# One opening, four visits: loads moved to GpSimd's queue, a bias load moved behind half of B, put-aside sums in A's tiles, and ten sums of B drawn forward

## The chip, the core and the metric

The kernel runs on one core of a Trainium2 chip. The metric is the device time of one execution in microseconds (us). The engines of the core have short names in the profile: PE is the matrix engine (PEld its weight loads), DVE the vector engine, ACT the scalar engine, POOL is GpSimd, SP is the sync engine, which here only issues DMAs. DMAs are issued by SP and by POOL, each on a queue of its own; the transfers of both queues run on the same 16 DMA engines of the core.

## What is computed

```python
def setup_inputs():
    m, k, n = 4096, 4096, 4096
    return {
        "a": np.random.randn(m, k).astype(np.float32),
        "b": np.random.randn(k, n).astype(np.float32),
        "bias": np.random.randn(n).astype(np.float32),
    }

def reference(a, b, bias):
    return np.tanh(np.matmul(a, b) + bias)
```

All three inputs are fp32. The kernel casts A and B to fp16 while they are loaded (a cast in a DMA is issued on POOL's queue) and accumulates in fp32.

## The kernel before

**Tiling.** The output is cut into four column stretches of 1024 (two halves j of 512) and into 32 row tiles of 128. K is 4096, cut in two halves h of 16 steps t each; a step is 128 deep. Most of the work is done by a seven-product scheme (`PRODUCTS`, `product`, L278): a pair of row tiles and the two halves of K and of the columns make a 2x2 block problem, and seven products of sums of A's quadrants (`asum`: s1, s2, s5, s6, s7) with sums of B's quadrants (`bsum`: d3, d1, d4, e6, e7, each in four blocks of four steps) replace eight. Work between the products is put by hand into numbered slots (`at_slot`, seven slots to an item); an engine runs its instructions in the order in which this program writes them.

**The opening.** The sums of B don't exist at the start, so the first eight row tiles (m 0 to 3 are `g0`, 4 to 7 are `g1`) of the first column stretch are multiplied plainly (`mm`, L425, 512 matmuls of 128x512) in four visits, so that PE can begin with what has landed. Eight PSUM banks hold `mb[m % 4, j]`.

1. Visit one: `g0`, steps 0 to 3 of the first half of K. A's piece for it is `first`, four loads of 128 KB, turned by PE (`turn_first`, L528) and copied out by DVE and ACT (L530). ACT puts the eight sums aside in `spill[0..3]` (`put_aside`, L461).
2. Visit two: `g1`, steps 0 to 7; A comes by `land` (L475, POOL's queue) and is turned by DVE (`turn_in`, L173). ACT puts the sums aside in `spill[4..7]`; DVE copies `spill[0..3]` back into PSUM (L571).
3. Visit three: `g0`, steps 4 to 15. ACT puts the sums aside, again in `spill[0..3]`; DVE writes `spill[4..7]` plus bias into PSUM (`add_bias`, L85, eight instructions). These are the first instructions that read the bias tile `bias_bc`.
4. Visit four (`second_visit`, slots -20 to -1): `g1` to its end (slots -20 to -9), with tanh and store (`end`, L596); ACT copies `spill[0..3]`, to which DVE has added the bias in slots -16 to -14, back into PSUM (L611); then `g0`, steps 16 to 31 (slots -8 to -1). The sums of B for the first items of the seven-product scheme, and the turned A of item 0, are made beside it on DVE. Slot 0 starts the first product of item 0.

**Queues.** POOL issues, in this order: `first` (4 DMAs); four single-step loads of b11 and b12 (t = 2, 3); `land` g1a0, g1a1 (8); block 1 of b11 and b12 (8); `land` g0b (4); block 2 (8); `land` g0x0, g0x1 (8); block 3 (8); `land` g1x0, g1x1 (8); `land` g1c 0 to 3 (16); the second half of B, b21 and b22, in the block order 2, 0, 1, 3 (32); `land` g0c (16); then A for items 0, 1, and so on (`load_nat`). The DMAs of this queue share eight semaphores in turn, so that each waits until the one eight before it has landed. SP issues at the start: four loads of t = 0, 1 of b11 and b12 in fp32 (`early_b`, 256 KB each), which DVE (L511) and ACT (L512) cast into the fp16 tiles, and then the bias, one row of 4 KB copied to 128 partitions (512 KB written, L260).

**Tiles that are shared.** A tile with a tag takes the place of the tile that had this tag before, once all that read it are done. `spill[0..3]` have the tags of e7's four blocks (`SPILL[0]`), `spill[4..7]` those of block 1 of d3, d1, d4, e6 (`SPILL[1]`; `early_b` has two of these before it). A's tiles of `g0` (`aq[m, 0]` and `aq[m, 1]`) lie in the pool `quads` under a11, a21, a12, a22, two each, which items 0 and 1 use after them.

**The sums of B, before.** d3, d1 of block 2 in slot -13; d4, e6 of block 2 in -12; d3, d1, d4 of block 0 in -11; d3 of block 3 in -8; e7 of block 0 in -7; e6 of block 0 in -6; e7 of block 2 in -5; d1, d4, e6 of block 3 in -3, -2, -1; d3 of block 1 and e7 of block 3 in 0; d1, d4, e6, e7 of block 1 in 2, 3, 5, 7.

Of the kernel before, what the change touches and what calls it, by code (L numbers as in the profile page):

```python
# [8 lines left out]
P = 128  # L9
QP = 32  # L10
NB = 512
NCW = 2 * NB
T = 16
TB = 4
# [3 lines left out]
fp32 = mybir.dt.float32  # L18
fp16 = mybir.dt.float16
# [29 lines left out]
SPILL = (  # L49
    [f"e7_{blk}" for blk in range(4)],  # L50
    [f"{i}_1" for i in ("d3", "d1", "d4", "e6")],
)
# [4 lines left out]
def kernel(  # L57
# [7 lines left out]
    nc = tc.nc  # L65
# [8 lines left out]
    bops = ctx.enter_context(tc.tile_pool(name="bops", bufs=1))  # L74
    quads = ctx.enter_context(tc.tile_pool(name="quads", bufs=2))
    sums = ctx.enter_context(tc.tile_pool(name="sums", bufs=3))
    wide = ctx.enter_context(tc.tile_pool(name="wide", bufs=8))
# [146 lines left out]
    bop, raw = {}, {}  # L224

    def new_bop(name, blk):
        bop[name, blk] = bops.tile([P, TB, NB], fp16, name=f"{name}_{blk}", tag=f"{name}_{blk}")
        return bop[name, blk]

    def load_b(dst, c, blk, h, j, t0=0, nt=TB, one=None):  # L230
        dx, dt = (1, QP) if h or blk else (TB, 1)
        off = b.offset + (h * T * QP + blk * TB * QP + t0 * dt) * N + c * NCW + j * NB
        if nt == 1:
            src = bass.AP(tensor=b.tensor, offset=off, ap=[[KQ * N, 4], [dx * N, QP], [1, NB]])
            (one or nc.gpsimd).dma_start(out=dst if one else dst[:, t0, :], in_=src)
            return
        for q in (0, 2, 1, 3):
            src = bass.AP(
                tensor=b.tensor, offset=off + q * KQ * N, ap=[[dx * N, QP], [dt * N, nt], [1, NB]]
            )  # L240
            nc.gpsimd.dma_start(out=dst[ds(q * QP, QP), ds(t0, nt), :], in_=src)  # L241

    def load_raw(name, c, blk):
        raw[name, blk] = wide.tile([P, TB, NB], fp16, name=name, tag="wide")
        load_b(raw[name, blk], c, blk, *((0, 1) if name == "b12" else (1, 0)))

    def load_op(name, c, blk):
        load_b(new_bop(name, blk), c, blk, *((0, 0) if name == "b11" else (1, 1)))
# [6 lines left out]
        x, y = (bop[i, blk] if (i, blk) in bop else raw[i, blk] for i in (x, y))  # L255
        tt(new_bop(name, blk), x, y, op)

    def load_bias(c):
        src = bias[ds(c * NCW, NCW)]
        nc.sync.dma_start(  # L260
            out=bias_bc, in_=bass.AP(tensor=src.tensor, offset=src.offset, ap=[[0, P], *src.ap])
        )

# [95 lines left out]
    def at_slot(slot, f, *args):  # L359
        work.setdefault(slot, []).append((f, args))  # L360
# [47 lines left out]
    def opening_b(names, blk, t0=0, nt=TB):  # L408
        for name in names:
            if t0 == 0:  # L410
                if name in ("b11", "b22"):
                    new_bop(name, blk)
                else:
                    raw[name, blk] = wide.tile([P, TB, NB], fp16, name=name, tag="wide")
            dst = bop[name, blk] if name in ("b11", "b22") else raw[name, blk]
            load_b(dst, 0, blk, int(name[1]) - 1, int(name[2]) - 1, t0, nt)
# [6 lines left out]
    def mm(m, j, kt, start=False, stop=False):  # L423
        h, t = divmod(kt, T)
        nc.tensor.matmul(  # L425
            mb[m % 4, j], aq[m, h][:, t, :], right(kt, j),
            start=start, stop=stop, skip_group_check=True,
        )

    def across(ms, k0, k1, fresh=False):  # L430
        for kt in range(k0, k1):
            for m in ms:
                for j in range(2):
                    mm(m, j, kt, fresh and kt == k0)

    def down(m, j, k0, k1, fresh=False, stop=False):
        for kt in range(k0, k1):
            mm(m, j, kt, fresh and kt == k0, stop and kt == k1 - 1)
# [6 lines left out]
    for m in g0:  # L445
        for h in range(2):
            name = f"a{m % 2 + 1}{h + 1}"
# [4 lines left out]
    spill = {}  # L452
# [7 lines left out]
    def put_aside(m, j):  # L460
        nc.scalar.copy(spill[m, j], mb[m % 4, j])  # L461

    def add_bias(m, j, to):
        tt(to, spill[m, j], bias_bc[:, ds(j * NB, NB)], ADD)
# [3 lines left out]
    def land(key, m, k0, nk, tag, nrow=1):  # L468

        h, t0 = divmod(k0, T)  # L470
        pool = sums if tag == "sum" else bops
        tl = pool.tile([P, 4 * nrow, nk * QP], fp16, name="land", tag=tag)
        for q in (0, 2, 1, 3):
            src = a[ds(m * P, nrow * P), ds(q * KQ + h * T * QP + t0 * QP, nk * QP)]
            nc.gpsimd.dma_start(  # L475
                out=tl[ds(q * QP, QP)], in_=src.rearrange("(mb p) k -> p mb k", p=QP)
            )
        landed[key] = (tl, m, k0, nk)
# [18 lines left out]
    for m in g0:  # L497
        src = a[ds(m * P, P), :].rearrange("p (q k) -> p q k", q=4)[:, :, ds(0, TB * QP)]
        nc.gpsimd.dma_start(out=first[:, m], in_=src)  # L499
    nc.gpsimd.affine_select(  # L500
        out=ident, in_=ident, compare_op=mybir.AluOpType.is_equal, fill=0.0,
        base=0, pattern=[[-1, P]], channel_multiplier=1,
    )
    early_b = [bops.tile([P, 2, NB], fp32, name="early_b", tag=SPILL[1][t]) for t in range(2)]
    new_bop("b11", 0)
    raw["b12", 0] = wide.tile([P, TB, NB], fp16, name="b12", tag="wide")
    for t in range(2):
        for j in range(2):
            load_b(early_b[t][:, j], 0, 0, 0, j, t, 1, nc.sync)
    for t in range(2):  # L510
        nc.vector.tensor_copy(bop["b11", 0][:, t], early_b[t][:, 0])  # L511
        nc.scalar.copy(raw["b12", 0][:, t], early_b[t][:, 1])  # L512
    for t in range(2, TB):
        opening_b(("b11", "b12"), 0, t, 1)
    land("g1a0", 4, 0, TP, "sum", 2)
    land("g1a1", 6, 0, TP, "sum", 2)
# [21 lines left out]
    def turn_pairs(key):  # L538
        for p in range(2):
            for r in range(2):  # L540
                turn_in(f"{key}{p}", r)
# [33 lines left out]
        down(m, j, TB, TP)  # L575
    turn_pairs("g0x")
    land(("g1c", 3), 7, T, T, LAND[1])
    for blk in H1:
        opening_b(("b21", "b22"), blk)
    load_bias(0)  # L580
    across(g0, TP, T - 2)
    turn_pairs("g1x")
    for m, j in rows4:
        down(m, j, T - 2, T, stop=True)
        put_aside(m, j)
        add_bias(4 + m, j, mb[m, j])

# [33 lines left out]
    for i, (m, j) in enumerate(rows4):  # L621
        at_slot(-16 + i // 3, add_bias, m, j, spill[m, j])
    for slot, name, blk in (
        (-13, "d3", 2), (-13, "d1", 2), (-12, "d4", 2), (-12, "e6", 2),
        (-11, "d3", 0), (-11, "d1", 0), (-11, "d4", 0), (-8, "d3", 3), (-7, "e7", 0),
        (-6, "e6", 0), (-5, "e7", 2), (-3, "d1", 3), (-2, "d4", 3), (-1, "e6", 3),
        (0, "d3", 1), (0, "e7", 3), (2, "d1", 1), (3, "d4", 1), (5, "e6", 1), (7, "e7", 1),
    ):
        at_slot(slot, bsum, name, blk)

# [3 lines left out]
    for c in range(1, NC):  # L634
        n = next(n for n in range(len(items)) if items[n][0] == c)
        change(c, 0, n - 2)
        change(c, 1, n - 1)
        at_slot(SLOTS * (n - 1) + 3, load_bias, c)
# [39 lines left out]
```

## Time and profile before

| what | value |
|---|---|
| median of 3 runs | 1601.43 us (1601.06 to 1601.47) |
| the profiled execution | 1598.97 us, of which its span is 1597.2 us |
| PE busy | 1571.0 us, 98% of the span, 7259 matmuls |
| DVE, ACT, POOL busy | 918.0, 268.6, 384.2 us (57%, 17%, 24%) |
| DMA on POOL's queue | 85.51 MB written, 36.5% of 16 engines' span |
| DMA on SP's queue | 173.05 MB, 33.0% |
| mean granted clock of PE | 0.993 |

A line of the timeline gives start, duration, engine, line, operation, tiles and a count, and in brackets the idle time of the engine ahead of it with what ended it. A line of the table of windows gives, for a stretch, the busy time and the number of instructions of PE, PEld, DVE, ACT and POOL, then the granted clock, the share of the DMA engines and GB/s written. The chain of waits is followed back from the last instruction; each piece is a start, a duration and what it was. Beside these views the trace has, for every DMA, the time at which each of the 16 DMA engines reported its part done; "landed" below is the last of these 16.

### The profile page before, as it was taken

Reading aid. Unit: us, or ns where it says so; the run is one execution under the profiler, and the core shown is the slowest. Engines: PE = TensorE matmul, PEld = TensorE weight load, DVE = VectorE, ACT = ScalarE, POOL = GpSimd, SP = SyncE. Lnnn points to the kernel's source line nnn. Section 1 sums busy time; section 2 is a strip of 40 time slices with the busy share of each in tenths; the row PEclk is TensorE's granted clock in tenths of the full one; section 3 lists DMA queues with packets and bytes.
Section 4 is the critical chain, followed back from the end, with each engine's and each line's share of the span. In section 5 each row is a group of like instructions: output and inputs, shape, how many; then the busy total and the mean of one; then the engine's idle time right before and its main releaser. Section 6 shows DMA issues by size and latency. Waiting matters only on the chain.

```text
span 1597.2 us, 18918 instructions
## 1 busy us (share of the span) xinstructions
PE 1571.0 (98%) x7259; PEld 710.3 (44%) x7259; DVE 918.0 (57%) x1044; ACT 268.6 (17%) x475; POOL 384.2 (24%) x721
## 2 busy tenths in 40 slices
PE   5998999999999999999999999999999999999998
PEld 2444444444444444444444444444444444444443
DVE  1769777777885665577795333333369433334332
ACT  1221111111221111111122111111122211111111
POOL 4765434364532221146441000000140000000000
PEclk7999999999999999999999999999999999999999
DMA  8999978899978765599996444444494444444441
GB/s 126 187 212 232 203 174 176 176 196 224 192 168 234 184 160 157 164 220 224 215 166 171 121 131 139 121 135 132 134 191 117 145 139 132 125 139 130 121 143 49
DMA packets 163114, 259.76 MB, mean 163 GB/s; under 512 B 24784, under 2 KB 83664, under 8 KB 163024
## 3 DMA queue, kind: packets, MB, share of 16 engines
q0 software_dynamic: 93376, 85.51, 36.5%
q1 hardware_dynamic: 69648, 173.05, 33.0%
q8 instruction: 57, 0.93, 0.2%
q14 instruction: 33, 0.27, 0.1%
HBM read 243.27 MB, written 100.66 MB: 215 GB/s over the span
## 4 chain that ended last, share of the span: by engine, by line
PE 93%; DMA 4%; POOL 1%; issue 1%; DVE 1%; ACT 0%; DVEq 0%; POOLq 0%
PE ps L278 90%; PE ps L425 3%; DMA nat<-in_a_dram 2%; DMA b<-in_b_dram 2%; POOL land L475 0%; POOL b L241 0%; DMA land<-in_a_dram 0%; POOL first L499 0%; DVE a L173 0%; DVE oa L173 0%; POOL nat L145 0%; ACT o L596 0%; ACT ps L611 0%; DVE s L85 0%; DVE d L85 0%
## 5 line engine op out<-in xcount | busy, mean ns | idle before, releaser
L278 PEld LDWEIGHTS <-a 128*128 128x128 f16 x3648 | 356.9, 98 | 433.4 <-issue 3.1
L278 PEld LDWEIGHTS <-s 128*128 128x128 f16 x3072 | 300.6, 98 | 364.0 <-issue 1.7
L278 PE MATMUL ps<-d,a 128*128 128x512 f16 x1920 | 434.0, 379 | 2.8 <-DVE ps L85 2.8
L278 PE MATMUL ps<-b,s 128*128 128x512 f16 x1920 | 434.0, 379 | 1.4 <-DVE s L85 1.4
L278 PE MATMUL ps<-e,a 128*128 128x512 f16 x1728 | 390.4, 379 | 0.0
L85 DVE TENSOR_TENSOR s<-a,a 128x2048 f16<-128x2048 f16 x192 | 233.1, 1215 | 13.1 <-DMA a<-scratch 12.1
L241 POOL DMA_DIRECT2D b<-in_b_dram x248 | 133.7, 547 | 434.4 <-PE ps L278 362.4
L145 POOL DMA_DIRECT2D nat<-in_a_dram x272 | 142.1, 534 | 314.1 <-DVE a L173 254.3
L278 PE MATMUL ps<-d,s 128*128 128x512 f16 x960 | 217.0, 379 | 0.0
L173 DVE STREAM_TRANSPOSE a<-nat 128x256 f16<-128x256 f16 (+2 forms) x244 | 205.4, 886 | 14.2 <-PE ps L278 8.7
L295 ACT ACTIVATE o<-ps 128x512 f32<-128x512 f32 x180 | 108.2, 601 | 310.0 <-issue 299.1
L85 DVE TENSOR_TENSOR ps<-cs,ps 128x512 f32<-128x512 f32 x60 | 41.4, 695 | 186.5 <-PE ps L278 186.5
L85 DVE TENSOR_TENSOR a<-a,a 128x2048 f16<-128x2048 f16 x108 | 131.5, 1217 | 0.0
L85 DVE TENSOR_TENSOR ps<-ps,s 128x512 f32<-128x512 f32 x72 | 49.4, 698 | 121.6 <-PE ps L278 112.7
L85 DVE TENSOR_TENSOR ps<-ps,bias_bc 128x512 f32<-128x512 f32 x60 | 41.8, 697 | 132.3 <-PE ps L278 132.3
L85 DVE TENSOR_TENSOR o<-ds,ps 128x512 f32<-128x512 f32 x60 | 41.2, 687 | 125.0 <-PE ps L278 89.5
L351 ACT ACTIVATE o<-o 128x512 f32<-128x512 f32 x60 | 37.8, 630 | 373.1 <-DVE o L85 373.1
L336 ACT COPY ds<-ps 128x512 f32<-128x512 f32 x60 | 35.1, 585 | 307.8 <-PE ps L278 307.8
L155 POOL DMA_DIRECT2D nat<-in_a_dram x128 | 68.6, 545 | 41.9 <-DVE a L173 25.5
L425 PE MATMUL ps<-b,oa 128*128 128x512 f16 x256 | 59.1, 391 | 3.6 <-ACT oa L530 1.7
L85 DVE TENSOR_TENSOR d<-b,b 128x2048 f16<-128x2048 f16 x48 | 57.5, 1221 | 0.1
L425 PE MATMUL ps<-b,ao 128*128 128x512 f16 x256 | 55.7, 379 | 0.3 <-DMA b<-in_b_dram 0.3
(42 smaller groups left out, 407.6 us busy)
## 6 DMA issues: line engine op xcount, KB each, us to landing
out_dram<-o SPq DMA_DIRECT2D x256, 256.0 KB, 4.0
a<-scratch SPq DMA_DIRECT2D x124, 512.0 KB, 4.5
nat<-in_a_dram POOLq DMA_DIRECT2D x272, 128.0 KB, 6.9
b<-in_b_dram POOLq DMA_DIRECT2D x252, 128.0 KB, 5.9
scratch<-a SPq DMA_DIRECT2D x48, 512.0 KB, 5.2
nat<-in_a_dram POOLq DMA_DIRECT2D x128, 64.0 KB, 4.5
scratch<-a SPq DMA_DIRECT2D x32, 256.0 KB, 6.3
land<-in_a_dram POOLq DMA_DIRECT2D x60, 128.0 KB, 5.1
```

The source lines that it names most:

```text
L85: nc.vector.tensor_tensor(out=out_, in0=in0, in1=in1, op=op)
L145: nc.gpsimd.dma_start(out=tl[ds(q * QP, QP), :, :], in_=src.rearrange("(mb p) k -> p mb k", p=QP),)
L155: nc.gpsimd.dma_start(out=tl[ds(q * QP, QP), :, h, :], in_=src.rearrange("(mb p) k -> p mb k", p=QP),)
L173: nc.vector.transpose(dst[:, ds(t, n), :].rearrange("P t (mb p) -> P mb t p", p=QP), src[:, :, ds(t * QP, n * QP)].rearrange(order, x=QP),)
L241: nc.gpsimd.dma_start(out=dst[ds(q * QP, QP), ds(t0, nt), :], in_=src)
L278: nc.tensor.matmul(st[where], at, bt, start=what == "m2" and i == 0, stop=i == len(ts_) - 1, skip_group_check=True,)
L295: nc.scalar.activation(o, src, TANH)
L336: nc.scalar.copy(st["ds"], st["d"])
L351: nc.scalar.activation(o, o, TANH)
L425: nc.tensor.matmul(mb[m % 4, j], aq[m, h][:, t, :], right(kt, j), start=start, stop=stop, skip_group_check=True,)
```

## The change

Three things.

1. `early_b` goes, with its four SP loads and its four casts. All four steps of block 0 of b11 and b12 are loaded by eight single-step DMAs on POOL's queue, behind `first`. The bias is loaded on POOL's queue too, between the last `land` of `g1c` and the first load of b21 and b22.
2. The sums of visit three are put aside in new tiles in `quads`, under a11 and a21 (the tile of row m takes the place of `aq[m, 0]`), instead of `spill[0..3]` under e7's tags.
3. Ten sums of B, not seven, stand ahead of slot -10: block 2 of all five, d3, d1, d4 of block 0 and e7 of blocks 0 and 1, from slot -14 on; the rest is drawn forward too.

```diff
-    def load_b(dst, c, blk, h, j, t0=0, nt=TB, one=None):
+    def load_b(dst, c, blk, h, j, t0=0, nt=TB):
...
-            (one or nc.gpsimd).dma_start(out=dst if one else dst[:, t0, :], in_=src)
+            nc.gpsimd.dma_start(out=dst[:, t0, :], in_=src)
...
-    def load_bias(c):
+    def load_bias(c, queue=nc.sync):
         src = bias[ds(c * NCW, NCW)]
-        nc.sync.dma_start(
+        queue.dma_start(
...
-    early_b = [bops.tile([P, 2, NB], fp32, name="early_b", tag=SPILL[1][t]) for t in range(2)]
-    new_bop("b11", 0)
-    raw["b12", 0] = wide.tile([P, TB, NB], fp16, name="b12", tag="wide")
-    for t in range(2):
-        for j in range(2):
-            load_b(early_b[t][:, j], 0, 0, 0, j, t, 1, nc.sync)
-    for t in range(2):
-        nc.vector.tensor_copy(bop["b11", 0][:, t], early_b[t][:, 0])
-        nc.scalar.copy(raw["b12", 0][:, t], early_b[t][:, 1])
-    for t in range(2, TB):
+    for t in range(TB):
         opening_b(("b11", "b12"), 0, t, 1)
...
     land(("g1c", 3), 7, T, T, LAND[1])
+    load_bias(0, nc.gpsimd)
     for blk in H1:
         opening_b(("b21", "b22"), blk)
-    load_bias(0)
     across(g0, TP, T - 2)
     turn_pairs("g1x")
     for m, j in rows4:
         down(m, j, T - 2, T, stop=True)
+        if j == 0:
+            tl = quads.tile([P, 2, NB], fp32, name="spill", tag=f"a{m % 2 + 1}1")
+            spill[m, 0], spill[m, 1] = tl[:, 0], tl[:, 1]
         put_aside(m, j)
         add_bias(4 + m, j, mb[m, j])
...
-        (-13, "d3", 2), (-13, "d1", 2), (-12, "d4", 2), (-12, "e6", 2),
-        (-11, "d3", 0), (-11, "d1", 0), (-11, "d4", 0), (-8, "d3", 3), (-7, "e7", 0),
-        (-6, "e6", 0), (-5, "e7", 2), (-3, "d1", 3), (-2, "d4", 3), (-1, "e6", 3),
-        (0, "d3", 1), (0, "e7", 3), (2, "d1", 1), (3, "d4", 1), (5, "e6", 1), (7, "e7", 1),
+        (-14, "d3", 2), (-14, "d1", 2), (-13, "d4", 2), (-13, "e6", 2), (-13, "e7", 2),
+        (-12, "d3", 0), (-12, "d1", 0), (-12, "d4", 0), (-11, "e7", 0), (-11, "e7", 1),
+        (-8, "d3", 3), (-8, "e7", 3), (-7, "d1", 3), (-7, "d4", 3), (-6, "e6", 0),
+        (-3, "e6", 3), (0, "d3", 1), (2, "d1", 1), (3, "d4", 1), (5, "e6", 1),
     ):
         at_slot(slot, bsum, name, blk)
```

## The prediction

> **What bounds it now.** First the page's chain by engine, then the chain in order of time:
>
> ```profile
> PE 93%; DMA 4%; POOL 1%; issue 1%; DVE 1%; ACT 0%; DVEq 0%; POOLq 0%
> ```
> ```profile
> 4.74 21.35 DMA b<-in_b_dram
> ...
> 29.71 6.71 DMA b<-in_b_dram
> ...
> 48.14 5.14 DMA land<-in_a_dram
> ...
> 55.83 48.10 PE ps L425 x222
> ...
> 148.88 1437.88 PE ps L278 x6662
> ```
>
> From 148.88 us on PE never waits until its last products, and the change leaves its matmuls alone; so only what moves PE ahead of 148.88 counts. Up to 55.83 the chain is POOL's queue and its DMAs. Next the timeline of the start, with its DMAs:
>
> ```profile
> 11.75 0.62 PE L528 MATMUL tp<-ident,first 128*128 128x128 f16 x4 [6.57 <-DMA first<-in_a_dram]
> ...
> 24.00 0.62 PE L528 MATMUL tp<-ident,first 128*128 128x128 f16 x4 [0.15 <-DMA first<-in_a_dram]
> ...
> 24.42 7.97 PE L425 MATMUL ps<-b,oa 128*128 128x512 f16 x28
> ```
> ```profile
> early_b<-in_b_dram SPq DMA_DIRECT2D x4, 256.0 KB
> ...
> first<-in_a_dram POOLq DMA_DIRECT2D x4, 128.0 KB, 16.2
> bias_bc<-in_bias_dram SPq DMA_DIRECT2D x1, 512.0 KB, 19.9
> ```
>
> PE waits for `first`, whose four loads land at 11.7, 17.0, 20.5 and 24.0. In the completion records 12 of the 16 DMA engines are done with them by 6.9, 8.0, 8.7 and 10.7; the other four are those that `early_b` runs on (each of its loads is reported by four engines alone, the last at 21.9). So SP's loads hold four engines, and POOL's queue, where every load waits for the one eight before it, stands still: the first `land` of g1a0 lands at 27.3. The last look is at the bias's first use, and at the rate and the clock (stretch, PE, PEld, DVE, ACT, POOL, granted clock, DMA share, GB/s):
>
> ```profile
> 66.33 4.87 DVE L85 TENSOR_TENSOR ps<-spill,bias_bc 128x512 f32<-128x512 f32 x8
> ...
> 68.36 41.60 PE L425 MATMUL ps<-b,ao 128*128 128x512 f16 x192
> ...
> 72.13 15.46 POOL L241 DMA_DIRECT2D b<-in_b_dram x24
> ```
> ```profile
> 4.08:7.50 3.42, 1.10 (x5) 0.29 (x3) 0.00 (x0) 0.00 (x0) 3.33 (x6) 1.00 1.23 154
> 7.50:28.00 20.50, 7.91 (x29) 3.01 (x30) 1.74 (x6) 2.43 (x6) 3.98 (x7) 0.50 0.80 123
> ...
> 72.00:88.00 16.00, 16.00 (x76) 7.25 (x75) 16.00 (x15) 0.00 (x0) 13.14 (x25) 1.00 1.21 194
> ...
> 147.40:150.80 3.40, 1.92 (x9) 0.87 (x9) 3.40 (x5) 0.00 (x0) 3.40 (x7) 1.00 0.80 113
> ```
>
> Visit four starts at 68.36, two us after DVE began to add a bias that had long landed (23.8). In the new place the bias stands in POOL's queue where b21's first load is now issued, at 72.13. That is the crux: the queue gets faster at its head, and the bias moves to its end.
>
> **Part one, the loads.** (a) *Head.* With SP idle all 16 engines go at the pace of the 12: `first` done by about 9.5. Then eight single-step loads, four more than before on POOL (0.70 us of issue each, 2.8 in all, under their DMAs). The records show what such a load costs: of the 12 free engines four finish the second one at 12.3 to 13.0, the other eight report already at 10.2 to 11.3. Each load lies on four engines, the next on four others. One has 128 rows, 32 to an engine, and 1 KB packets take 98 ns: 3.1 us, and about 0.4 for each of the three loads of which an engine has nothing: 4.3 us for four. Two rounds: 9.5 + 8.6 = 18.1. One more load behind that: g1a0's first piece at 19.0 (18.5 to 19.6), 8.3 us sooner than 27.3.
> (b) *The queue from there to the bias.* 67 more loads of 128 KB. Before, they took from 27.34 to 76.38 (the last of g1c): 49.0. At the steady 194 GB/s of the window above each takes 131,072 / 194,000 = 0.676, 45.3 in all; the difference lies in two slow stretches (31 to 36 and 62 to 71), each just behind a time when POOL had stood still. The first such pause goes, the second (1.66 us of "issue" at 61.05) has no releaser that the change touches. I take the middle, 47.2; both ends go into the range.
> (c) *The bias.* 512 KB, uncast, on POOL's queue: no row. From below its 128 packets of 4 KB, which took 172 ns undisturbed, eight to an engine: 1.4 us. From above 512 KB at 194 GB/s: 2.7. No gain is possible where it is added to the queue. I take 1.6, nearer to the row of the same packets. It lands at 19.0 + 47.2 + 1.6 = 67.8.
> (d) *Who waits.* The first `add_bias` on DVE, 0.13 behind a landing as the transposes at 50.75 are; 0.70 for it and 0.05 to PE: visit four starts at 68.7. Behind it on DVE stand seven more (4.2 us) and the four transposes of g1c (8.9): 68.0 + 4.9 + 8.9 = 81.8; PE needs them in slot -16, 13.8 us after its start, 82.5. Just covered; if not, the rest is a stall.
> (e) *PE in between.* Visits one to three have 32, 64 and 96 matmuls of 0.216 us and get their tiles 8 us sooner: b's steps land by 18.1, visit one ends near 24, visit two near 38, visit three, which waits for g0x (42.6) and its turning behind DVE's eight copies, near 59. So PE idles 8 to 10 us ahead of the bias.
> (f) *The clock.* The rows show full clock withdrawn after a stretch of 3.4 us with 1.10 busy, and kept with 1.92; back at 28.0 after one full stretch (24.57 to 28.00 is all busy). An idle of 8 us therefore costs the clock, and PE runs at half for the rest of the stretch in which it restarts, or for one more: 1.7 to 5.1 us, half of it lost: 0.85 to 2.6, taken as 1.7.
>
> Visit four is then worth a start at 68.7 + 1.7 = 70.4 against 68.36: **2.0 us later.** The casts that go (two of 0.43 on DVE, two of 0.62 on ACT) stood beside waits for `first` and were on no path.
>
> **Parts two and three.** The new tile of row m takes the place of `aq[m, 0]`, which PE reads through row (m, 1); the first copy aside then waits two matmuls more, 0.43 us. DVE waits for the bias longer than that; were the bias there, DVE's first sum would end 67.5, still ahead of 68.36. The tiles are read out by slot -9 and items 0 and 1 want a11 and a21 from slot -6 on. Ten sums of 1.17 us ahead of slot -10 are 3.5 us more there than seven. Their cover is DVE's wait of 8.41 us for g0c at 101.14, kept by a queue that runs some 9 us sooner behind the bias. Without the cover they would be done at 98 and, with g0c's turns behind them, still ahead of slot -8 (112). Nor do they gain: at the start of item 0 PE waits 1.45 us at 142.49 and 2.78 at 148.88. DVE's order between the second and third product there (a sum over a21, d1 of block 1, s1, two transposes, then the sum PE waits for: 142.35 to 148.83) is the same after. No sum of B that goes from slots 0 and 7 stands in it. I cost both parts at zero; bounds: 2.8 lost if the transposes slip behind the bias, 2.8 gained if that wait went.
>
> **The sum.** 1598.97 of the profiled execution + 2.0 = 1601.0; the median of the runs lies 2.46 above the profiled one, so **1603.4**. Bounds of the start: 18.5 + 45.3 + 1.4 + 0.9 = 66.1, with 0.85 of clock 1.4 sooner than now; 19.6 + 49.0 + 2.7 + 0.9 = 72.2, with 2.6 of clock 6.4 later. So 1600.0 to 1607.8.
>
> **Rivals.**
> *A, slower: both slow stretches stay and the bias is dear.* They were there before, but followed pauses of POOL of which one goes. Place: the first `add_bias`. Price 3.2 to 6.4, 1606 (middle). It decides from a bias that lands after 69.0 (69.0 + 0.9 + 1.7 = 71.6 against 68.36 is 3.2).
> *B, slower: the head doesn't get faster.* If the pace were the engines' total work and not the four that SP's loads sit on, g1a0's first piece would stay at 27.3, the bias land at 27.3 + 49.0 + 1.6 = 77.9 and visit four start at 78.8 with 1.7 of clock: 12.1 later, 1613.5. The 12 engines that were done with `first` by 10.7, while PE waited till 24.0 for the other four, speak against it. The Trainium skill's page "DMA: Bandwidth & Descriptors", section "Rules for kernel authors", is on this side: spreading DMAs over SP, ACT and GpSimd doesn't help bandwidth, since all run on the same 16 engines. By that rule the sum would be 1613.5.
> *C, faster: the bias is in time.* If the single-step loads spread better than (a) and the queue keeps its steady pace, the bias lands by 62, PE starts by 63, and an idle of 3 us may keep the clock: 5.4 sooner, 1596. For it: DMA share 1.2 and more for most of the way. Against it: the four-engine pattern, and a queue that never ran 67 loads without a slow stretch.
>
> **How the numbers follow.** Forecast 0.57, A 0.24, B 0.07, C 0.12. What a measurement can't tell from no change is 0.2%, 3.2 us: 1598.2 to 1604.6. The forecast's own values reach above that in about 0.08. Slower 0.08 + 0.24 + 0.07 = 0.39, faster 0.12, same 0.49. The range 1599.5 to 1608 takes in the bounds above with A and leaves out B and C, 0.19. Its low end is 0.5 under the low bound.
>
> **What would show it.** (a) `first` landed by 10, g1a0's first transposes near 21 instead of 29.49. (b, c) The bias issued near 62, landed 65 to 71. (d) DVE's first sum with `bias_bc` released by a DMA, and PE's `ao` matmuls of visit four right behind it, at 66 to 72. (e, f) PE idle for several us ahead of it, its clock 0.50 for 2 to 5 us. Parts two and three: the waits of about 1.45 and 2.8 us behind item 0's first two products still there. It is wrong if visit four starts without a wait for the bias, if the clock stays full, or if PE waits anew between 72 and 140.

## The result, and the profile after

The changed kernel takes 1603.22 us (median of 12 runs, 1601.26 to 1604.41) against 1600.50 for the kernel before on the same chip (12 runs, 1598.05 to 1601.47): a ratio of 1.0021 over all these runs, with a 95% interval of 1.0013 to 1.0029 (the two medians alone give 1.0017). The profiled execution took 1602.83 us, its span 1600.8, with a mean granted clock of 0.994. Behind the lines of `early_b` the line numbers are nine lower than before (`turn_first` is L519 and its copies L521); those ahead of them are unchanged (`first` is L499, a single-step load of B L235).

The chain of waits by engine, and its pieces in order of time (start, duration, what):

```profile
PE 94%; DMA 3%; POOL 2%; issue 1%; DVE 0%; ACT 0%; POOLq 0%; DVEq 0%
```
```profile
8.15 8.72 DMA b<-in_b_dram
...
61.62 6.07 DMA bias_bc<-in_bias_dram
67.78 0.71 DVE ps L85
68.53 65.12 PE ps L425 x292
...
150.98 1439.54 PE ps L278 x6662
```

Before, the chain came to visit four out of PE's own work, at 55.83. Now it comes out of POOL's queue: the bias is issued at 61.62 and lands at 67.68, DVE adds it, and PE starts visit four at 68.53. The piece in which PE never waits again starts at 150.98 instead of 148.88. The timeline of the opening (start, duration, engine, line, operation, tiles, count, idle ahead and its releaser; the last group of an engine is counted only as far as the view goes):

```profile
1.33 3.09 POOL L499 DMA_DIRECT2D first<-in_a_dram  x4 [0.82 <-POOLq L656]
...
5.08 0.90 PE L519 MATMUL tp<-ident,first 128*128 128x128 f16 x8
...
10.56 0.38 PE L425 MATMUL ps<-b,oa 128*128 128x512 f16 x1 [4.58 <-DMA b<-in_b_dram]
...
14.29 7.97 PE L425 MATMUL ps<-b,oa 128*128 128x512 f16 x28
...
20.43 2.49 DVE L173 STREAM_TRANSPOSE ao<-land 128x512 f16<-128x512 f16 x4 [6.68 <-DMA land<-in_a_dram]
...
45.43 12.69 PE L425 MATMUL ps<-b,oa 128*128 128x512 f16 x58 [0.52 <-DVE oa L173]
...
67.78 4.91 DVE L85 TENSOR_TENSOR ps<-spill,bias_bc 128x512 f32<-128x512 f32 x8 [10.77 <-DMA bias_bc<-in_bias_dram]
...
68.53 13.74 PE L425 MATMUL ps<-b,ao 128*128 128x512 f16 x54 [10.41 <-DVE ps L85]
...
72.60 8.88 DVE L173 STREAM_TRANSPOSE ao<-land 128x2048 f16<-128x2048 f16 x4
```

The 28 matmuls that began at 24.42 begin at 14.29: the head of the opening is ten us faster. What PE waits for there is no longer `first` but the single-step loads. All of the ten us is spent again ahead of 68.53, where PE stands still for 10.41 us until DVE has its bias. The DMAs of the first 20 us show where the head is faster (queue, count, KB each, median us from issue to landing); the reason is tested below:

```profile
first<-in_a_dram POOLq DMA_DIRECT2D x4, 128.0 KB, 3.3
```

It was 16.2. By the completion records `first` lands at 4.53, 5.52, 6.26 and 7.58, the eight single-step loads from 10.43 to 17.74, and the first `land` of g1a0 at 18.34 (27.34 before). Then the clock, in the windows (stretch, PE, PEld, DVE, ACT, POOL, granted clock, DMA share, GB/s):

```profile
10.98:17.81 6.83, 5.61 (x20) 2.54 (x20) 0.49 (x2) 0.65 (x2) 3.31 (x7) 0.50 1.28 160
62.18:72.42 10.24, 3.89 (x10) 1.37 (x10) 4.64 (x8) 0.00 (x0) 7.54 (x14) 0.50 1.17 209
147.55:150.97 3.42, 0.65 (x3) 0.20 (x2) 3.42 (x7) 0.00 (x0) 1.53 (x3) 1.00 1.03 211
150.97:154.38 3.41, 3.40 (x9) 1.20 (x9) 3.41 (x6) 0.00 (x0) 2.14 (x5) 0.50 0.94 231
```

Behind visit one PE loses its full clock twice: from 62.2 to 72.46, of which it works 68.53 to 72.46 at half speed, and once more from 150.97 to 154.38, behind a stretch of 3.42 us in which it was busy for 0.65. The second is seen in the start of item 0's products (the timeline of PE, first of the kernel before, then of the changed one):

```profile
137.42 3.62 PE L278 MATMUL ps<-b,s 128*128 128x512 f16 x16
142.49 3.61 PE L278 MATMUL ps<-b,s 128*128 128x512 f16 x16 [1.45 <-DVE s L85]
148.88 3.61 PE L278 MATMUL ps<-d,a 128*128 128x512 f16 x16 [2.78 <-DVE ps L85]
```
```profile
139.52 3.62 PE L278 MATMUL ps<-b,s 128*128 128x512 f16 x16
144.58 3.61 PE L278 MATMUL ps<-b,s 128*128 128x512 f16 x16 [1.45 <-DVE s L85]
150.98 5.28 PE L278 MATMUL ps<-d,a 128*128 128x512 f16 x16 [2.78 <-DVE ps L85]
```

The two waits of 1.45 and 2.78 are the same as before. The third product, of 16 matmuls like the two ahead of it, takes 5.28 us instead of 3.61: 1.67 lost to the clock. So the spans differ by 3.6 us (1600.8 − 1597.2), of which 2.1 are there when item 0 starts (139.52 against 137.42) and 1.7 come with the second loss of the clock; 0.2 is won elsewhere.

### The profile page after: what moved, and what is told of

Read it like the earlier page. It is cut to its first block, busy times and chain, and to the rows that moved or that the text cites. A ratio compares the mean times of both kernels' runs of the same rounds, so it can differ in the third digit from the quotient of the medians.

```text
span 1600.8 us, 18906 instructions
## 1 busy us (share of the span) xinstructions
PE 1573.5 (98%) x7259; PEld 711.6 (44%) x7259; DVE 917.5 (57%) x1042; ACT 267.5 (17%) x473; POOL 387.5 (24%) x726
## 4 chain that ended last, share of the span: by engine, by line
PE 94%; DMA 3%; POOL 2%; issue 1%; DVE 0%; ACT 0%; POOLq 0%; DVEq 0%
PE ps L278 90%; PE ps L425 4%; DMA b<-in_b_dram 1%; DMA nat<-in_a_dram 1%; POOL land L475 1%; DMA land<-in_a_dram 1%; POOL b L241 1%; DMA bias_bc<-in_bias_dram 0%; POOL b L235 0%; POOL first L499 0%; POOL nat L145 0%; DVE ps L85 0%; DVE a L173 0%; DVE o L85 0%; ACT o L351 0%
```

## The experiments

Theory one is that of the prediction: the loads make the head faster, the bias at the end of the queue takes that back and somewhat more, the tiles and the sums do nothing. Each run was compared with runs of the kernel before on the same chip.

**The bias back on SP** (`e1_bias_sp`: the changed kernel with one line taken back). It asks what the other parts are worth without the wait.

```diff
-    load_bias(0, nc.gpsimd)
+    load_bias(0)
```

> The changed kernel with the bias on SP's queue again, all else as changed. Theory one (the bias's late landing is what costs): the bias lands in the first 20 us, visit four starts where PE is done with visit three (58.1 in the changed kernel's profile, so 58.6), the clock stays full: 9.9 + 2.0 = 11.9 us sooner than the changed kernel, 1591.3, 0.9943 of before. Theory two (the queue's total work bounds the opening, whichever load stands where): the wait comes back at b21's or g1c's landing inside visit four, a gain of 5 us or less against the changed kernel, 1598 to 1603. Theory three (the put-aside tiles and the sums of B are what costs): no faster than before, 1600 to 1603.

Measured: 1589.43 us, ratio 0.9938 (0.9926 to 0.9951). The bias lands at 5.25, and the timeline has visit four without a wait:

```profile
54.76 4.01 ACT L461 COPY spill<-ps 128x512 f32<-128x512 f32 x8 [18.66 <-PE ps L425]
56.25 4.87 DVE L85 TENSOR_TENSOR ps<-spill,bias_bc 128x512 f32<-128x512 f32 x8
57.15 5.13 PE L425 MATMUL ps<-b,ao 128*128 128x512 f16 x23
```

DVE adds the bias while ACT is still putting sums aside, and visit four starts at 57.15 instead of 68.53. So the place of the bias in the queue alone costs 11.4 us of start, and turns a gain of 0.6% into a loss of 0.2%.

**Part one's loads alone** (`e2_loads_only`: the kernel before without `early_b`; the bias stays on SP).

```diff
-    early_b = [bops.tile([P, 2, NB], fp32, name="early_b", tag=SPILL[1][t]) for t in range(2)]
...
-    for t in range(2, TB):
+    for t in range(TB):
         opening_b(("b11", "b12"), 0, t, 1)
```

> Before with the four early loads moved to POOL's queue and nothing else (bias on SP, put-aside tiles and sums of B as before). Theory one: the same as the run with the bias back on SP, 1591 within 1 us, since the other two parts cost and bring nothing. Theory three: faster than that run by what the two parts cost, 2 to 3 us. A fourth: e7's tiles are needed sooner in a quicker opening, so without the put-aside tiles DVE waits for ACT and it is 1 to 4 us slower than that run.

Measured: 1588.94 us, 0.9934 (0.9921 to 0.9946), the same as the run above within the intervals. Within the intervals all of the gain is the loads' own.

**Why they gain** (`e11_early_b_16_engines`: the kernel before, with each SP load of `early_b` cut in four, so that 32 partitions are its outermost dimension instead of 4). Bytes and queue stay as they were, SP issues 16 loads of 64 KB instead of 4 of 256. If the transfers of the second queue cost by their total work (the prediction's rival B), this changes nothing; if by the four engines on which they sit, it should gain nearly what taking them away gains.

```diff
-            (one or nc.gpsimd).dma_start(out=dst if one else dst[:, t0, :], in_=src)
+            for q in range(4) if one else ():
+                src = bass.AP(tensor=b.tensor, offset=off + q * KQ * N, ap=[[dx * N, QP], [1, NB]])
+                one.dma_start(out=dst[ds(q * QP, QP)], in_=src)
+            if not one:
+                nc.gpsimd.dma_start(out=dst[:, t0, :], in_=src)
```

> Before with the four early fp32 loads still on SP's queue, but each cut into four loads of 32 rows, whose outermost dimension is 32 instead of 4; nothing else changed, the same bytes on the same queue. Theory one (four engines are held): A's first piece is no longer held, its last load lands by 11 instead of 24, g1a0's first piece by 18 instead of 27.3, visit four starts near 59 instead of 68.4: 1590 to 1593, 0.993 to 0.995 of before. The rival (POOL's queue is slow because SP's bytes share the engines with it): no more than 2 us gained, 0.999 to 1.

Measured: 1592.36 us, 0.9949 (0.9937 to 0.9962). The DMA issues of its first 30 us:

```profile
early_b<-in_b_dram SPq DMA_DIRECT2D x16, 64.0 KB, 4.7
first<-in_a_dram POOLq DMA_DIRECT2D x4, 128.0 KB, 5.1
```

`first` lands from 4.94 to 9.74 with all of SP's megabyte beside it (11.7 to 24.0 before), the first piece of g1a0 at 17.61, and visit four starts at 59.08. So what held POOL's queue was not that a second queue moved data, but that each of that queue's loads lay on four engines.

**The bias alone** (`e3_bias_only`: the kernel before with only the bias moved).

```diff
     land(("g1c", 3), 7, T, T, LAND[1])
+    load_bias(0, nc.gpsimd)
     for blk in H1:
         opening_b(("b21", "b22"), blk)
-    load_bias(0)
```

> Before with the bias moved on POOL's queue behind the last load of g1c and nothing else. Theory one: the head of the queue stays as slow as before (g1a0's first piece near 27), the bias lands near 78, visit four starts near 78.9 instead of 68.36 and at half clock for about 4 us: 12.5 slower than before, 1613. Theory two: with 512 KB gone from the head, the head lands about 4 us sooner, so 8 slower, 1608.5.

Measured: 1610.65 us, 1.0073 (1.0060 to 1.0085): 11 us slower. Visit four, in its timeline:

```profile
78.09 4.91 DVE L85 TENSOR_TENSOR ps<-spill,bias_bc 128x512 f32<-128x512 f32 x8 [13.40 <-DMA bias_bc<-in_bias_dram]
...
78.84 16.38 PE L425 MATMUL ps<-b,ao 128*128 128x512 f16 x64 [12.85 <-DVE ps L85]
```

The start at 78.84 was expected at 78.9. With the bias off SP the first piece of g1a0 landed 2.4 us sooner (24.93), yet the bias landed at 78.00 all the same. This is also about what the whole change would have come to if its loads had made nothing faster (rival B's price was 12.1 us).

**The tiles and the sums alone** (`e4_tiles_and_sums`: parts two and three on the kernel before).

```diff
+        if j == 0:
+            tl = quads.tile([P, 2, NB], fp32, name="spill", tag=f"a{m % 2 + 1}1")
+            spill[m, 0], spill[m, 1] = tl[:, 0], tl[:, 1]
...
-        (-13, "d3", 2), (-13, "d1", 2), (-12, "d4", 2), (-12, "e6", 2),
+        (-14, "d3", 2), (-14, "d1", 2), (-13, "d4", 2), (-13, "e6", 2), (-13, "e7", 2),
```

> Before with the put-aside tiles in A's place and the ten sums of B, loads and bias as before. Theory one: nothing, within 1 us of before; the waits of 1.45 and 2.78 us behind item 0's first two products are still there. Theory three: slower by the change's whole 2.7 us.

Measured: 1600.46 us, 1.0007 (0.9998 to 1.0016). Its timeline of PE at item 0:

```profile
142.52 3.61 PE L278 MATMUL ps<-b,s 128*128 128x512 f16 x16 [1.45 <-DVE s L85]
148.91 4.93 PE L278 MATMUL ps<-d,a 128*128 128x512 f16 x16 [2.78 <-DVE ps L85]
```

Both waits are there and begin within 0.03 us of the kernel before. Yet here, too, the third product runs at half clock (148.2 to 151.6), and this profiled span is 1.5 us longer than that of before (1598.7 against 1597.2). The same waits at the same times lose the clock in one execution and keep it in another.

**Part one without the other two** (`e5_part_one_only`: the changed kernel with the list of sums and the put-aside tiles of before).

```diff
-        if j == 0:
-            tl = quads.tile([P, 2, NB], fp32, name="spill", tag=f"a{m % 2 + 1}1")
-            spill[m, 0], spill[m, 1] = tl[:, 0], tl[:, 1]
...
-        (-14, "d3", 2), (-14, "d1", 2), (-13, "d4", 2), (-13, "e6", 2), (-13, "e7", 2),
+        (-13, "d3", 2), (-13, "d1", 2), (-12, "d4", 2), (-12, "e6", 2),
```

> The changed kernel with the put-aside tiles and the order of the sums of B as before, so that only the loads and the bias have moved. Theory one: as the changed kernel, 1.0021 of before within 0.001, visit four at 68.5. Theory three (tiles and sums cost): as before, 1.000.

Measured: 1603.90 us, 1.0016 (1.0008 to 1.0025). In its profile, the slowest of its 11 runs, the bias landed at 70.37 and visit four started at 71.21, not at 68.5: five loads of POOL's queue between 24 and 62 us landed 1.4 to 2.0 us behind the one ahead of them, against three of 1.3 to 2.0 in the changed kernel. The ratio agrees with that of the whole change within the intervals. Part one is the whole effect, as far as these runs can tell.

**The wait filled with matmuls** (`e6_filled_wait`: the changed kernel with 38 matmuls over zeros into `mb[3, 1]` ahead of its last `add_bias`, which writes that bank anew). It prices the half clock of visit four.

```diff
-        add_bias(4 + m, j, mb[m, j])
+        add_bias(4 + m, j, mb[m, j]) if (m, j) != (3, 1) else None
+    for i in range(38):
+        nc.tensor.matmul(mb[3, 1], zeros[:, :P], zeros, start=i == 0, stop=i == 37, skip_group_check=True)
+    add_bias(7, 1, mb[3, 1])
```

> The changed kernel with 38 matmuls of zeros (8.2 us at full clock) put on PE between visit three and visit four, into the bank that is filled last, so that PE's clock is not withdrawn while it waits for the bias; the output is the same. Theory one: visit four still starts at 68.5, its 64 matmuls run at 0.216 us from the first on, and the end is 2.0 us sooner than the changed kernel (0.85 to 2.6), 1.0009 of before. If the clock's record costs nothing, or the zeros don't hold it: as the changed kernel, 1.0021. If the filling overruns the bias: later than that.

Measured: 1600.83 us, 1.0004 (0.9995 to 1.0012). The timeline of PE and the windows:

```profile
59.50 8.36 PE L582 MATMUL ps<-zeros 128*128 128x512 f16 x38 [1.51 <-ACT spill L461]
67.70 17.65 PE L425 MATMUL ps<-b,ao 128*128 128x512 f16 x81
```
```profile
60.00:68.00 8.00, 8.00 (x39) 3.64 (x38) 1.12 (x2) 0.00 (x0) 6.05 (x12) 1.00 1.20 234
68.00:76.00 8.00, 8.00 (x39) 3.60 (x38) 8.00 (x9) 0.00 (x0) 6.62 (x13) 1.00 1.24 201
```

The clock stays at 1.00 through the wait, and the time is back at that of the kernel before. The bias landed 0.9 us sooner in this profile (66.79), so the 1.7 thousandths between the two ratios, some 2.7 us with intervals of more than 1 us each way, hold more than the 1.97 of the clock.

**Block 0 in four-step loads** (`e7_block_loads`: the changed kernel with block 0 loaded like the other blocks, in eight loads of four steps whose outermost dimension is 32 partitions).

```diff
-    for t in range(TB):
-        opening_b(("b11", "b12"), 0, t, 1)
+    opening_b(("b11", "b12"), 0)
```

> The changed kernel with block 0 of b11 and b12 in eight four-step loads like the other blocks (outermost dimension 32), instead of eight single-step loads (outermost dimension 4), in the same place of the queue. Theory one (a single-step load lies on four engines): eight loads of 0.65 behind the last piece of A at 7.6, so block 0 is there at 12.8 instead of 17.7 and g1a0's first piece at 13.5 instead of 18.3; the bias lands 4.8 sooner, near 62.9, visit four starts near 63.7 and 5 us are gained on the changed kernel: 0.999 of before. If it is the number of the loads and their bytes that counts: no change, 1.0021.

Measured: 1601.19 us, 1.0004 (0.9996 to 1.0013). Right in its sign, half as large as expected: block 0 was there at 15.42 (17.74 in the changed kernel, 12.8 expected), g1a0's first piece at 16.13, the bias at 65.27, visit four at 66.11. Eight such loads at 0.65 us each should take 5.2 us; here they took 7.9 behind `first`: 2.0 to the first landing and 1.9 between two later ones (10.27 and 12.17), with no cause that the trace shows.

**The same with the bias on SP** (`e8_block_loads_bias_sp`: both edits).

> The same block loads with the bias on SP's queue at the start. Theory one: what PE waits for ahead of visit four is then g0x and DVE's turning of it, 4 us sooner in the queue but behind DVE's eight copies, so 0 to 3 us sooner than the run with the bias back on SP (0.9938 of before): 0.992 to 0.994. If the wait moves to b21 or to g1c in visit four: no gain over that run.

Measured: 1591.06 us, 0.9945 (0.9933 to 0.9957). A miss: it isn't faster than the run with single-step loads (0.9938). The second product of item 0 starts at 133.32 against 131.51 there. What it loses is seen at its start, in its timeline of PE:

```profile
12.51 0.59 PE L425 MATMUL ps<-b,oa 128*128 128x512 f16 x1 [5.77 <-DMA b<-in_b_dram]
15.70 0.58 PE L425 MATMUL ps<-b,oa 128*128 128x512 f16 x1 [2.61 <-DMA b<-in_b_dram]
...
17.79 6.38 PE L425 MATMUL ps<-b,oa 128*128 128x512 f16 x25
```

A load of four steps brings a quarter of each step, so PE has its first tile of B when four of the eight have landed and its second only when all have, at 15.7. The single-step loads take longer for the block but let PE begin with its first step: the long run of matmuls that starts at 17.79 here starts at 14.77 in `e1_bias_sp`. The reading, from one profile of each: with the bias at the queue's end the queue's total decides; with the bias away, PE's own start does.

**The wait of 2.78 taken out** (`e9_first_products`: `e1_bias_sp` with d1 of block 1, s1 and s6 of item 0 moved ahead of the sum that PE waits for, and the turns of item 1's a21 one slot later).

```diff
-            turns = (("a22", (0, 0)), ("a21", (2, 2)), ("a11", (3, 4)), ("a12", (5, 5)))
+            if n == 1:
+                turns = (("a22", (0, 0)), ("a21", (3, 3)), ("a11", (3, 4)), ("a12", (5, 5)))
...
-        at_slot(s0 + 9, asum, n, "s1")
-        at_slot(s0 + (12 if late else 8), asum, n, "s6")
+        at_slot(s0 + (9 if n else 7), asum, n, "s1")
+        at_slot(s0 + (12 if late else 8 if n else 7), asum, n, "s6")
...
-        (-3, "e6", 3), (0, "d3", 1), (2, "d1", 1), (3, "d4", 1), (5, "e6", 1),
+        (-3, "e6", 3), (0, "d3", 1), (0, "d1", 1), (3, "d4", 1), (5, "e6", 1),
```

> The run with the bias back on SP, and DVE's work around item 0's first products put in another order: d1 of block 1, s1 and the sum over a21 ahead of the first product instead of behind it, the two transposes of item 1's a21 in slot 3 instead of 2. Theory one: DVE stood idle for 3.53 us ahead of the first product's sum, so the three fit; the sum that PE waits for then begins as the second product ends, and the wait shrinks from 2.78 to about 0.8 us, too short for the clock to be withdrawn (1.7): 2 to 3.7 us sooner than the run with the bias back on SP, 0.9915 to 0.9925 of before. If the wait isn't set by that order: 0.9938.

Measured: 1585.97 us, 0.9911 (0.9897 to 0.9924). The timeline of PE at item 0:

```profile
131.97 3.61 PE L278 MATMUL ps<-b,s 128*128 128x512 f16 x16 [1.45 <-DVE s L85]
...
136.37 3.61 PE L278 MATMUL ps<-d,a 128*128 128x512 f16 x16 [0.79 <-DVE ps L85]
```

The wait is 0.79, as expected, and the third product keeps its full speed (3.61, against 5.27 in the profile of `e1_bias_sp`); the mean granted clock is 0.998, the span 1584.4. The ratio is a little below the range that was expected, which its interval reaches. This is the fastest version of the study.

**The head's wait filled too** (`e10_filled_head`: `e9_first_products` with 20 more matmuls over zeros ahead of the first row of visit one).

```diff
     turn_first(1, nc.scalar.copy)
+    fill(20, NB)
     row(0)
```

> The same with 20 matmuls of zeros (4.3 us) between the second turning of A and the first real matmul, where PE waits 5 us for block 0 of B with the clock withdrawn until 15.0. Theory one: the first 32 matmuls run at full clock, visit one ends 1.4 us sooner, and of this what g0x's transposes don't take back reaches the end: 0 to 1.4 us, 0.9905 to 0.992 of before.

Measured: 1586.46 us, 0.9914 (0.9901 to 0.9928): nothing gained. The clock is full from 3.9 us to the end, but PE, now faster through visit one, waits where it did not before (its timeline):

```profile
6.59 4.48 PE L493 MATMUL warm<-zeros 128*128 128x512 f16 x20
...
20.57 7.30 PE L427 MATMUL ps<-b,ao 128*128 128x512 f16 x33 [0.25 <-DVE ao L173]
...
28.64 6.85 PE L427 MATMUL ps<-b,ao 128*128 128x512 f16 x31 [0.78 <-DMA b<-in_b_dram]
```

The stretch at half speed in the head stood beside loads that decide anyway.

## Why the prediction held, point by point

- **(a) The head.** Right in its steps: g1a0's first piece landed at 18.34, 0.16 ahead of the bounds. That it came so near is in part luck, since terms were off and cancelled: `first` was done at 7.58, not 9.5; the eight single-step loads took 10.2 us behind it, not 8.6; the load behind them took 0.6, not 0.9. That each lies on four engines, and that two rounds of four follow, agrees with the completion records; but the first round ended 6.5 us behind `first` and the second 3.7 behind the first, not 4.3 each. Rival B, that the head would not get faster, is refuted twice: by the loads alone (0.9934), and by the run that cut SP's loads over more engines (0.9949). The Trainium skill's rule that stood on its side ("DMA: Bandwidth & Descriptors", "Rules for kernel authors") is about bandwidth and doesn't speak of a DMA that holds a few engines. The same section says that an outermost dimension of fewer than 16 confines a DMA to at most that many engines, and this case agrees: with 4 outermost in SP's loads, four engines alone report each of them, and `first` took until 24.0; with 32 outermost, until 9.74.
- **(b) The queue.** 47.76 us for the 67 loads against 47.2 taken. That is the middle of two bounds, and so no test of the reason given for it: slow stretches did stay (32.47 to 34.44 and 56.44 to 58.26, each one load), but neither stands just behind a pause of POOL, as the prediction had it. Their places differ from run to run, and their cause stays open.
- **(c) The bias.** 1.58 us behind the last load of g1c, against 1.6; it landed at 67.68, against 67.8.
- **(d) Who waits.** DVE's first sum at 67.78 and visit four at 68.53, against 68.7. The transposes of g1c ended at 81.48 and PE did not wait for them: no cover was lost.
- **(e) PE idle.** 10.41 us, a little over the 8 to 10.
- **(f) The clock.** 3.93 us at half, 1.97 lost, against 1.7. The run with filled waits shows that the loss hangs on the wait: no half clock there, and the time of the kernel before.
- **Parts two and three.** Nothing, as costed (1.0007 alone; 1.0016 without them against 1.0021 with them). The two waits stay.
- **Rivals A and C.** A needed the bias to land after 69.0; it landed at 67.68, though in the profile of part one alone it landed at 70.37, so the queue does reach A's place in some executions. C was the right sum for another kernel: with the bias in time (`e1_bias_sp`) the time is 1589.43, even below C's 1596, since PE's own work in visits one to three sets the start, at 57, and not a bias at 62.

**What the prediction had not seen.** Item 0 starts 2.10 us later, against 2.0; but the profiled execution came out at 1602.83 instead of 1601.0. The difference is the second loss of the clock, 1.67 us behind a wait that the prediction had listed and left as it was. It looked at that wait for a change of its length and not for its place against the clock's stretches. Before, the wait of 2.78 straddled two of them: the prediction's own row has the second, 1.92 of 3.40 busy, and the first (windows) was

```profile
144.00:147.40 3.40, 2.10 (x10) 0.88 (x9) 3.40 (x6) 0.00 (x0) 0.05 (x1) 1.00 1.09 284
```

After, the whole wait fell into one. This loss isn't the change's own: of the eleven profiled executions that have this wait of 2.78, nine lose the clock behind it, the run of the tiles and sums among them, which has PE at the same times as the kernel before; only the one profile of the kernel before and that of `e8_block_loads_bias_sp` keep it. So the kernel before probably loses it in most of its executions too, which one profile of it can't show.

**What was luck.** The sum added to 2.0 us the profiled execution of before, which had kept its clock at item 0, and the distance of 2.46 to the median of three runs, 1601.43. The median of the twelve runs is 1600.50, and from that the sum would have been 1602.5. By the medians the change costs 2.7 us (3.2 by the means). A base 0.9 too high and a cost 0.7 too small make up the agreement of 1603.4 with 1603.22; the mechanism, and the start of visit four to 0.2 us, were right without that.

## What to carry to other kernels

A faster head of a queue is worth only what stands behind it in that queue: before something is moved to the end of the queue, find its first reader, and compare the reader's new time, not the old one, with the time of landing. Here 512 KB that had been waiting unnoticed on the other queue used up ten us of gain, and taking back that one line made the kernel 0.6% faster than before. A DMA whose outermost dimension is 4 takes four engines and holds up every load of the other queue that shares them; look for engines that report late in the completion records before blaming the bandwidth.

## What the runs showed of the hardware

**The clock is judged in fixed stretches.** All changes of the granted clock are multiples of 3.41 us apart (10.98 to 17.81 is two, 62.2 to 72.46 three, 150.97 to 154.38 one), at times that differ from run to run. The Trainium skill's page "TensorE: Matmul & The Clock Gate" ("Part 1: The HAM clock gate", "What's actually happening") gives a free-running window of 3413 ns, and the trace agrees. Its table has the clock drop after an idle window; here a window that was busy for 0.65 of 3.42 us was enough, and the measurement decides. Behind item 0's second product the clock went after stretches that were busy for 0.63 to 1.35 of some 3.41 us (nine profiles) and stayed after 1.44 (`e8_block_loads_bias_sp`) and 2.10 (before). In the head of `e1_bias_sp` it went after one with 1.59, so PE's busy time alone doesn't give the limit. A wait of 2.78 us therefore cost 1.3 to 1.7 us more or nothing, by where it fell, and a wait of 0.79 cost nothing. 38 matmuls over zeros kept the clock at 1.00 through a wait of 8.4 us.

**Single-step loads on POOL's queue are dear beyond their issue.** Eight of 128 KB took 10.2 us to land behind `first`, 1.27 each, at 0.67 to 0.73 us of issue. In `e7_block_loads`, with 32 partitions outermost, eight loads of the same bytes took 7.9 and landed 0.61 to 0.72 us apart but for one gap (9.55, 10.27, 12.17, 12.82, 13.51, 14.12, 14.77, 15.42).

**512 KB of bias behind the last load of g1c landed 1.58 us after it**, and 1.47 to 2.18 in the four other runs that have it there: less than the 2.7 that the queue's 194 GB/s would make of it.
